# A diffusion transformer block in one kernel: the first MLP's latent tokens by Strassen's seven block products as well, the seven in a new order, and the sums of the second weights made inside each MLP

## The chip, the cores and the metric

The kernel runs on one core of a Trainium2 chip. The metric is device microseconds from start to end of one execution; three executions of the kernel before took 3232.7 to 3236.72 us, with a median of 3235.53. A profile of one execution (3236.36 us; its span from the first to the last instruction is 3234.6 us) gives the durations used below.

## The reference

Two layers work on 1024 latent tokens and 256 context tokens of width 1024, in fp32. Layer 0 mixes tokens by a long convolution and a windowed attention, layer 1 by latent attention and a Fourier mix. Behind each mixer comes an MLP, and only layer 0 goes on with the context:

```python
def _mlp(h, w1, w2):
    return jnp.square(jax.nn.relu(h @ w1)) @ w2

xl = _layer_norm(ALPHA * xl + g1 * yl, ln_g[l, 0], ln_b[l, 0])
xl = _layer_norm(ALPHA * xl + g2 * _mlp(_modulate(xl, sh2, sc2), mlp_w1[l], mlp_w2[l]), ln_g[l, 1], ln_b[l, 1])
if need_ctx:
    ...
    xc = _layer_norm(ALPHA * xc + g2c * _mlp(_modulate(xc, sh2c, sc2c), mlp_w1[l], mlp_w2[l]), ln_g[l, 1], ln_b[l, 1])
```

`w1` is 1024 x 4096 and `w2` 4096 x 1024. The gates and shifts come from `silu(c) @ mod_w[l]`, rows of 6 x 1024.

## The kernel before, in words

Every fp32 product is made of three TensorE passes on operands split in a high and a low part (`split`, L162 and L163: ScalarE rounds the high part, VectorE subtracts it for the low one; `mm3`, L169 to L171: high by high, low by high, high by low, into one PSUM bank). So each tile that TensorE reads costs ScalarE and VectorE one operation each.

Order: layer 0's mixer, `mixer_out` (output projection, residual, layer norm, tile by tile of 128 tokens), `Mlp`/`mlp`, layer 1's mixer (`MixerIn`, `mixer_cd_in`, `mla`), `mixer_out`, `FastMlp`. The instructions of each engine stand roughly in the order in which the program emits them; transfers are issued by SP (`nc.sync`) and by GpSimd (`nc.gpsimd`), each a queue in order. A tile pool with n buffers makes the writer of tile n+1 wait for the last reader of tile 1.

*The first MLP* (`mlp`, L1392) is plain. Its ten token tiles (eight latent, two context) go in two groups of five. For each group and each pair of 128-wide slices of the hidden width it loads and splits a slice of `w1` and of `w2`, makes the first layer with 320 moving columns (two halves of 640 tokens, 24 matmuls each), squares the relu, and makes the second layer with 512 columns for each token tile and half of the output, which VectorE adds up in SBUF (L1474). Beside it, `weight_sums` (L1547) makes four block sums of layer 1's `w2` for the second MLP and stores them to DRAM (`tsums`), and `mod_rows` (L348) builds layer 1's modulation, 128 multiply-adds on VectorE with their weights loaded by SP. Two steps before its end it makes `MixerIn`, which loads and splits the next mixer's weights, and `ahead` starts that mixer's projection between the last token tiles (`AHEAD`).

*The second MLP* (`FastMlp`, L1590) treats each matrix as 2 x 2 blocks and makes each 2 x 2 product by seven products instead of eight. The tokens' blocks are b11 to b22 and their sums t1 to t4 (`token_sums`), the weights' are a11 to a22 and s1 to s4. Its first layer goes by pairs of 128-wide hidden slices (`pairs`, L1734): 16 pairs, seven items each; an item is one split block of weights (128 x 512) and 12 matmuls of 512 columns. Three PSUM banks collect a pair's products, `a`, `x` and `y`; where a later item adds to a bank, VectorE has read it first. For the first `EARLY` = 7 pairs the items a11 b11 and a12 b21 are made ahead of all (`first`), while the token sums are still being formed; their results go to DRAM and are loaded again by the pair. `Stream` splits operands ahead of the multiplications, as far as a ring of `RING` = 6 places allows. Each pair ends with the squares and their four sums, all stored to DRAM (`sums`). The second layer (`passes`, L1844) goes product by product over the whole hidden width: seven times 16 items of 12 matmuls on four banks, one for each 128 tokens of a half, its operands loaded from `sums` and from `tsums` or `w2`. Residual and layer norm of each token half are put between the items (`aside`); the last product is finished tile by tile (`tail`).

Of the kernel before, what the change touches and what calls it, by code (L numbers as in the profile page):

```python
# [38 lines left out]
AHEAD = (1, 3, 4)  # L39
RING = 6  # L40
EARLY = 7
# [187 lines left out]
def setup(k, es):  # L229
# [23 lines left out]
    k.tsums = [dr.tile([128, 4, 2, 512], F32, name=f"tsums{j}") for j in range(8)]  # L253
    k.first = [dr.tile([128, 512], F32, name=f"first{j}") for j in range(EARLY)]
    k.erp = dr.tile([NH, 8, 31, 24], F32, name="erp")
# [455 lines left out]
def first_stage(k, hp, er):  # L711
# [4 lines left out]
    with ExitStack() as es:  # L716
# [27 lines left out]
        for j in range(1, 24):  # L744
# [24 lines left out]
            if extra and j in MODS:  # L769
                i, part = extra.pop(0)  # L770
                mod_rows(k, 0, i, 2, mr, ma, ph, "ph", cols=512, parts=(part,))
# [502 lines left out]
def mixer_out(k, l, y_of, weights, tiles, load_res, dst, streams, m):  # L1274
# [4 lines left out]
    with ExitStack() as es:  # L1279
        P = lambda n, b, **kw: es.enter_context(tc.tile_pool(name=n, bufs=b, reuse_waits="tile", **kw))  # L1280
        rw, rp = P("o_rw", 1), P("o_r", 2)
        if callable(weights):
            rs, sm, yb, w0, ya, w1, wr = P("o_rs", 2), P("o_sm", 4), P("o_yb", 1), P("o_w0", 1), P("o_ya", 1), P("o_w1", 1), P("o_wr", 4)
# [3 lines left out]
        else:  # L1287
            ya, yb, sm, rs = P("o_ya", 1), P("o_yb", 1), P("o_sm", 4), P("o_rs", 2)
# [3 lines left out]
        for t in tiles:  # L1292
# [20 lines left out]
            if t == tiles[-1]:  # L1313
                m.head()
# [8 lines left out]
class Mlp:  # L1323


    def __init__(self, k, es, l, src, groups, streams):
        self.k, self.l, self.src, self.groups, self.streams = k, l, src, groups, streams
        R = lambda e, n, b: e.enter_context(k.tc.tile_pool(name=n, bufs=b, reuse_waits="tile", side="right"))
        self.nmax = max(len(g) for g in groups) * 128
        self.xp, self.tmp = R(es, "m_x", 3), R(es, "m_tmp", 1)  # L1330
        self.pt = es.enter_context(k.tc.tile_pool(name="m_pt", bufs=2, space=PSUM, reuse_waits="tile"))
        self.first = es.enter_context(ExitStack())
        self.wp1, self.hp = R(self.first, "m_w1", 2), R(self.first, "m_h", 1)
        self.R = R
        self.scsh = None
        self.hs, self.fed, self.ready = {}, [], []

    def runs(self, gi):

        k, g = self.k, self.groups[gi]  # L1340
        if self.scsh is None:
            self.scsh = [mod_sc_sh(k, self.l, 1, s) for s in range(self.streams)]
        if gi not in self.hs:
            self.hs[gi] = [[self.hp.tile([128, self.nmax], F32R, tag=f"{p}{i}", name="m_" + p) for i in range(KT)] for p in ("hi", "lo")]
        runs = []
        for t in g:
            s = 0 if t < 8 else 1
            if not runs or runs[-1][0] != s or len(runs[-1][1]) == 2:
                runs.append((s, []))
            runs[-1][1].append(t)  # L1350
        return runs

    def normed(self, t, src=None):

        nc = self.k.nc
        x = self.xp.tile([128, D], F32, tag="mx", name="mx")
        if src is None:
            nc.gpsimd.dma_start(out=x, in_=self.src[t])
        ln_apply(self.k, x, x if src is None else src, self.k.co[0, t])
        return x  # L1360

# [23 lines left out]
    def head(self):  # L1385
        pass
# [1183 lines left out]
```

## Time and profile before

| | us |
|---|---|
| median of three executions | 3235.53 |
| lowest, highest | 3232.7, 3236.72 |
| profiled execution | 3236.36 |
| its span | 3234.6 |
| TensorE busy in it | 3122.5 (97%) |
| VectorE busy in it | 2294.5 (71%) |
| ScalarE busy in it | 1429.5 (44%) |

| stretch, us | what runs |
|---|---|
| 880 to 1007 | output projection of layer 0's mixer |
| 1007 to 1910 | first MLP |
| 1910 to 1990 | its last tiles, start of layer 1's mixer |
| 2488 to 2587 | output projection of layer 1's mixer |
| 2587 to 2640 | second MLP: items made ahead, token sums |
| 2640 to 2906 | its pairs |
| 2906 to 3235 | its second layer and the end |

PE is TensorE's matmuls, PEld its weight loads, DVE is VectorE, ACT ScalarE, POOL GpSimd. Matmuls are recorded with their whole passage, so neighbours overlap; the pace is read from start to start. An idle engine costs nothing unless TensorE waits for it.

### The profile page before, as it was taken

Reading aid. Unit: us, or ns where it says so; the run is one execution under the profiler, and the core shown is the slowest. Engines: PE = TensorE matmul, PEld = TensorE weight load, DVE = VectorE, ACT = ScalarE, POOL = GpSimd, SP = SyncE. Lnnn points to the kernel's source line nnn. Section 1 sums busy time; section 2 is a strip of 40 time slices with the busy share of each in tenths; the row PEclk is TensorE's granted clock in tenths of the full one; section 3 lists DMA queues with packets and bytes.
Section 4 is the critical chain, followed back from the end, with each engine's and each line's share of the span. In section 5 each row is a group of like instructions: output and inputs, shape, how many; then the busy total and the mean of one; then the engine's idle time right before and its main releaser. Section 6 shows DMA issues by size and latency. Waiting matters only on the chain. (4 is left out here: it accounts for less than half of the span.)

```text
span 3234.6 us, 47247 instructions
## 1 busy us (share of the span) xinstructions
PE 3122.5 (97%) x17700; PEld 2671.1 (83%) x17700; DVE 2294.5 (71%) x4231; ACT 1429.5 (44%) x2917; POOL 334.8 (10%) x525
## 2 busy tenths in 40 slices
PE   8999998999999999999999999999999999999998
PEld 4888886887778899888989987888888777888887
DVE  6777765888687777558555477687777886665668
ACT  3443333555543332235333334566666254444452
POOL 2100001222121000002000013100000212210001
PEclk9999998999999999999999999999999999999999
DMA  7434445332256676434434233200003355446564
GB/s 259 144 123 143 140 160 165 95 118 84 92 187 201 212 232 210 144 104 153 139 100 124 84 119 116 92 12 13 17 16 119 119 188 190 156 156 218 210 240 155
DMA packets 308786, 449.06 MB, mean 139 GB/s; under 512 B 26981, under 2 KB 208011, under 8 KB 308044
## 3 DMA queue, kind: packets, MB, share of 16 engines
q1 hardware_dynamic: 279004, 345.42, 33.1%
q0 software_dynamic: 29552, 100.62, 8.9%
q8 instruction: 139, 2.28, 0.3%
q14 instruction: 91, 0.75, 0.1%
HBM read 343.36 MB, written 104.26 MB: 138 GB/s over the span
## 5 line engine op out<-in xcount | busy, mean ns | idle before, releaser
L170 PE MATMUL mm<-m_lo,w1h 128*128 128x320 f32 x1024 | 316.7, 310 | 0.1
L169 PE MATMUL mm<-m_hi,w1h 128*128 128x320 f32 x1024 | 316.8, 310 | 0.0
L171 PE MATMUL mm<-m_hi,w1l 128*128 128x320 f32 x1024 | 316.1, 309 | 0.7 <-DVE w1l L163 0.7
L169 PE MATMUL mm<-w2h,ah 128*128 128x512 f32 x640 | 257.3, 402 | 10.4 <-DVE acc L1474 10.4
L171 PE MATMUL mm<-w2h,al 128*128 128x512 f32 x640 | 250.9, 392 | 0.0
L170 PE MATMUL mm<-w2l,ah 128*128 128x512 f32 x640 | 250.4, 391 | 0.0
L1474 DVE TENSOR_TENSOR acc<-mm,acc 128x512 f32<-128x512 f32 x270 | 183.9, 688 | 88.1 <-PE mm L171 86.9
L169 PE MATMUL pj<-hTh,hwh 128*128 128x512 f32 (+1 forms) x576 | 208.2, 362 | 0.0
L170 PE MATMUL pj<-hTl,hwh 128*128 128x512 f32 (+1 forms) x576 | 206.8, 360 | 0.3 <-DVE hTl L220 0.3
L171 PE MATMUL pj<-hTh,hwl 128*128 128x512 f32 (+1 forms) x576 | 206.6, 359 | 0.3 <-DVE hwl L163 0.3
L314 DVE SCALAR_TENSOR_TENSOR modacc<-modraw,silu,modacc 128x512 f32<-128x512 f32 x224 | 160.9, 747 | 47.5 <-DMA modraw<-in_mod_w 47.1
L169 PEld LDWEIGHTS mm<-m_hi,w1h 128*128 128x128 f32 x1024 | 192.2, 188 | 2.6 <-ACT m_hi L219 0.5
L170 PEld LDWEIGHTS mm<-m_lo,w1h 128*128 128x128 f32 x1024 | 192.2, 188 | 2.2 <-DVE m_lo L220 0.6
L171 PEld LDWEIGHTS mm<-m_hi,w1l 128*128 128x128 f32 x1024 | 192.1, 188 | 1.3 <-DVE w1l L163 1.0
L162 ACT CAST w2h<-wraw 128x1024 fp32r<-128x1024 f32 x64 | 64.5, 1047 | 265.7 <-PE mm L171 262.5
L163 DVE TENSOR_TENSOR w1l<-wraw,w1h 128x1024 fp32r<-128x1024 f32 x64 | 78.4, 1224 | 119.1 <-ACT w1h L162 119.0
L169 PEld LDWEIGHTS mm<-w2h,ah 128*128 128x128 f32 x640 | 120.8, 189 | 35.5 <-DVE acc L1474 14.6
L163 DVE TENSOR_TENSOR m_pl<-m_sl,m_ph 128x512 fp32r<-128x512 f32 x104 | 71.7, 690 | 101.0 <-ACT m_ph L162 101.0
L171 PEld LDWEIGHTS mm<-w2h,al 128*128 128x128 f32 x640 | 120.5, 188 | 25.3
L170 PEld LDWEIGHTS mm<-w2l,ah 128*128 128x128 f32 x640 | 120.9, 189 | 20.7
L2399 ACT ACTIVATE a_p<-a_s,a_m 128x512 f32<-128x512 f32 (+1 forms) x192 | 116.1, 614 | 44.2 <-DVE a_m L2395 43.5
L162 ACT CAST w1h<-wraw 128x1024 fp32r<-128x1024 f32 x64 | 67.1, 1049 | 138.6 <-PE mm L170 71.8
(1317 smaller groups left out, 9096.5 us busy)
## 6 DMA issues: line engine op xcount, KB each, us to landing
wraw<-in_mlp_w SPq DMA_DIRECT2D x128, 512.0 KB
modraw<-in_mod_w SPq DMA_DIRECT2D x160, 256.0 KB
m_sl<-sums SPq DMA_DIRECT2D x56, 512.0 KB
m_w<-in_mlp_w SPq DMA_DIRECT2D x39, 512.0 KB
m_ts<-in_mlp_w SPq DMA_DIRECT2D x16, 1024.0 KB
tsums<-m_ts POOLq DMA_DIRECT2D x16, 1024.0 KB, 5.0
sums<-m_s POOLq DMA_DIRECT2D x64, 256.0 KB, 3.7
m_sr<-tsums SPq DMA_DIRECT2D x32, 512.0 KB
```

Of the source, the lines that this page charges most:

```text
L162: nc.scalar.copy(hi, src)
L163: nc.vector.tensor_tensor(out=lo, in0=src, in1=hi, op=ALU.subtract)
L169: t.matmul(out, lh, rh, start=start, stop=False, skip_group_check=on)
L170: t.matmul(out, lh, rl, start=False, stop=False, skip_group_check=on)
L171: t.matmul(out, ll, rh, start=False, stop=stop, skip_group_check=on)
L314: k.nc.vector.scalar_tensor_tensor(out=acc, in0=w, scalar=c, in1=acc, op0=ALU.mult, op1=ALU.add)
L1474: nc.vector.tensor_tensor(out=acc[t][:, e], in0=ps, in1=acc[t][:, e], op=ALU.add)
L2399: nc.scalar.activation(out=p_[:, s:s + n], in_=ss[i][:, :n], func=AF.Exp, bias=m, scale=-1.0, accum_out=acc[:, i:i + 1])
```

## The change

The class `Mlp` with `mlp` and the function `weight_sums` are removed; `FastMlp` serves both layers. For layer 0 the latent tokens go through the seven products; the context's first layer is plain (256 columns), its squares and their block sums go to DRAM (`sumc`), and its second layer joins the seven products as a fifth token tile. In the pairs an item s1 t1 opens bank `y` (behind a11 b11 on `a` where that was not made ahead) and s4 b22 adds to it (behind a12 b21 on `a`); s2 t2, s3 t3 and a22 t4 go to `x`. The lists `five`, `three`, `six`, `seven` and `four` hold these, and a pair's `six`, `seven`, `four` alternate with the next pair's `five` and `three`. The seven products of the second layer follow the order of `PRODUCTS`. Each MLP makes its own sums of `w2`, in half units of 128 x 4 x 256 on the buffers of the token tiles, between its pairs. `EARLY` goes from 7 to 6. In `mixer_out` for layer 0 the residual's pools move to the right side of SBUF, and the weights' and operands' pools are closed at the last tile, where `head` opens the ring in their place. Layer 1's modulation is put between the context's steps and the first products of the second layer; `MixerIn` is made 13 items before the end.

```diff
-AHEAD = (1, 3, 4)
-EARLY = 7
+EARLY = 6
...
 def mod_rows(k, l, j, streams, raw_pool, acc_pool, pp, tag, tags=("wraw", "modacc"), cols=D, parts=(0, 1)):
...
                 mac(k, acc[s], w, k.silu[:, kt, s:s + 1], kt == 0)
+                yield True
...
 def mixer_out(k, l, y_of, weights, tiles, load_res, dst, streams, m):
-            rs, sm, yb, w0, ya, w1, wr = P("o_rs", 2), P("o_sm", 4), P("o_yb", 1), P("o_w0", 1), P("o_ya", 1), P("o_w1", 1), P("o_wr", 4)
+            rw, rp, rs, sm = (P(n, b, side="right") for n, b in (("o_rw", 1), ("o_r", 2), ("o_rs", 2), ("o_sm", 4)))
+            Q = lambda n, b: ops.enter_context(tc.tile_pool(name=n, bufs=b, reuse_waits="tile"))
+            wr, ya, yb, w0, w1 = Q("o_wr", 4), Q("o_ya", 1), Q("o_yb", 1), Q("o_w0", 1), Q("o_w1", 1)
...
             if t == tiles[-1]:
+                ops.close()
                 m.head()
...
-PRODUCTS = ("a11 b11", "a12 b21", "s2 t2", "s3 t3", "a22 t4", "s1 t1", "s4 b22")
+PRODUCTS = ("a11 b11", "a12 b21", "s1 t1", "s4 b22", "s2 t2", "s3 t3", "a22 t4")
+OPENS = (0, 2, 4)
...
+    def weight_sums(self):
+        k, tt = self.k, self.k.nc.vector.tensor_tensor
+        w2 = k.mlp_w2[self.l].rearrange("(j t p) (d c n) -> j c p t d n", t=2, p=128, d=2, c=2)
+        for j in range(FF // 256):
+            for c in range(2):
+                w = self.xp.tile([128, 4, 256], F32, tag="mx", name="m_ts")
+                for t in range(2):
+                    k.nc.sync.dma_start(out=w[:, 2 * t:2 * t + 2], in_=w2[j, c, :, t])
+                b11, b12, b21, b22 = (w[:, i] for i in range(4))
+                for out, a, b in ((b11, b12, b11), (b12, b22, b12), (b22, b22, b11), (b21, b21, b22)):
+                    tt(out=out, in0=a, in1=b, op=ALU.subtract)
+                    yield True
+                k.nc.gpsimd.dma_start(out=k.tsums[self.l][j // 2][:, :, j % 2, c * 256:c * 256 + 256], in_=w)
...
+                count[0] += 1
+                self.aside(1 + (count[0] % 3 == 0))
...
+            def after5():
+                if early:
+                    p.e, p.c = new("e"), new("c")
+                    nc.sync.dma_start(out=p.e, in_=k.first[j])
+                    nc.sync.dma_start(out=p.c, in_=k.sums[0, j // 2][:, j % 2])
+                p.f, p.g = new("f"), new("g")
+                add(p.f, p.y, p.e)
...
-        ps[0].six()
-        for j, p in enumerate(ps):
-            for f in p.front:
-                f()
-            if j + 1 < len(ps):
-                ps[j + 1].six()
-            for f in p.back:
-                f()
+        items = ps[0].five + ps[0].three
+        for p, q in zip(ps, ps[1:]):
+            items += p.six + q.five + p.seven + q.three + p.four
+        return items, ps[-1]
...
+            def multiply(*ws):
+                state[odd] = self.bank("c")
+                for i, w in enumerate(ws):
+                    h, l_ = (p.rearrange("p (k m) -> p k m", k=4) for p in w)
+                    for kt in range(4):
+                        mm3(k, state[odd][:, :LC], h[:, kt], l_[:, kt], self.xch[:, i * 4 + kt], self.xcl[:, i * 4 + kt], i + kt == 0, i + kt == 4)
+                        weave(k)
...
+        def multiply(i, j, m, a, b, *c):
+            if m < 4:
+                s = slice(m * 128, (m + 1) * 128)
+                h, l_ = a[0][:, s], a[1][:, s]
+            else:
+                h, l_ = c[0]
+            mm3(k, banks[m], h, l_, *b, i in OPENS and j == 0, j == nj - 1, i not in OPENS)
+            weave(k)
...
+        self.add(p.six + follow[:1] + p.seven + follow[1:2] + p.four)
+        self.hook(first_done)
+        self.add(follow[2:])
+        n = -(FF // 256) + 3 if self.then else 0
+        self.add(second[:n or None] if self.ctx else second[2:])
+        if self.then:
+            self.hook(next_stage)
+            self.add(second[n:])
...
+        for i in range(nm):
+            if i % 2 == 0:
+                self.ahead()
+            for _ in self.ends[i]:
+                pass
```

## Rows read from the trace of the kernel before

**Rows 1.** Page, part 1: busy us of an engine, share of the span, instructions.

```profile
PE 3122.5 (97%) x17700; PEld 2671.1 (83%) x17700; DVE 2294.5 (71%) x4231; ACT 1429.5 (44%) x2917; POOL 334.8 (10%) x525
```

**Rows 2.** Table by stretch, first MLP: stretch, length, busy of each engine (count), clock, DMA.

```profile
1007.00:1910.00 903.00, 891.73 (x5072) 810.41 (x5072) 577.30 (x845) 319.52 (x584) 37.52 (x50) 1.00 0.47 151
1030.00:1330.00 300.00, 291.78 (x1648) 264.30 (x1647) 210.96 (x310) 101.09 (x178) 10.69 (x15) 0.99 0.65 215
1910.00:1990.00 80.00, 71.85 (x343) 59.95 (x342) 71.98 (x181) 36.95 (x91) 27.83 (x47) 0.96 0.44 140
```

**Rows 3.** Table by stretch, second MLP.

```profile
2587.00:2630.00 43.00, 41.49 (x190) 33.59 (x188) 35.50 (x58) 25.54 (x49) 10.15 (x17) 1.00 0.66 208
2630.00:2640.00 10.00, 7.48 (x30) 5.96 (x29) 10.00 (x18) 6.14 (x11) 1.08 (x2) 0.83 0.25 97
2640.00:2740.00 100.00, 91.47 (x385) 72.56 (x384) 72.40 (x118) 41.61 (x72) 18.89 (x35) 0.98 0.61 195
2740.00:2906.00 166.00, 166.00 (x724) 135.62 (x723) 110.24 (x173) 83.04 (x139) 33.48 (x62) 1.00 0.46 154
2906.00:3200.00 294.00, 294.00 (x1296) 242.67 (x1295) 180.86 (x281) 136.16 (x241) 9.41 (x16) 1.00 0.62 217
```

**Rows 4.** Timeline of TensorE, first MLP: start us, duration us, instruction.

```profile
1201.18 0.31 PE L169 MATMUL mm<-m_hi,w1h 128*128 128x320 f32 x1
...
1201.91 0.31 PE L171 MATMUL mm<-m_hi,w1l 128*128 128x320 f32 x1
```

**Rows 5.** Timeline of TensorE, matmuls of 256 columns.

```profile
229.35 0.28 PE L521 MATMUL f_h<-f_w3h,f_hid 128*128 128x256 f32 x1
...
229.82 0.28 PE L169 MATMUL f_z<-tab_fwlh,f_sdh 128*128 128x256 f32 x1
```

**Rows 6.** Page, part 5, first MLP's matmuls: busy us, mean ns, idle before.

```profile
L170 PE MATMUL mm<-m_lo,w1h 128*128 128x320 f32 x1024 | 316.7, 310 | 0.1
...
L169 PE MATMUL mm<-w2h,ah 128*128 128x512 f32 x640 | 257.3, 402 | 10.4 <-DVE acc L1474 10.4
```

**Rows 7.** Waits of TensorE, first MLP: us in total, times, longest us.

```profile
PE mm L169 <- DVE acc L1474: 10.4, 7, 3.4
```

**Rows 8.** Waits of TensorE, second MLP.

```profile
PE m_x L169 <- DVE m_v L1799: 8.1, 5, 2.7
```

**Rows 9.** Chain that ended last, second MLP: start us, us, what.

```profile
2627.02 0.60 DVE m_t32l L163
...
2692.78 5.06 DMA m_e<-first
```

**Rows 10.** Page, part 6: transfers, KB of one, median us to landing.

```profile
m_ts<-in_mlp_w SPq DMA_DIRECT2D x16, 1024.0 KB
tsums<-m_ts POOLq DMA_DIRECT2D x16, 1024.0 KB, 5.0
```

**Rows 11.** Instruction groups 900 to 1960: busy us, mean ns, idle before.

```profile
L314 DVE SCALAR_TENSOR_TENSOR modacc<-modraw,silu,modacc 128x512 f32<-128x512 f32 x112 | 81.2, 748 | 29.9 <-DMA modraw<-in_mod_w 29.7
...
L189 DVE BATCH_NORM_STATS2 bnst<-ra 128x6 f32<-128x512 f32 x76 | 49.1, 682 | 0.2
...
L220 DVE TENSOR_TENSOR m_lo<-modtmp,m_hi 128x256 fp32r<-128x256 f32 x32 | 13.5, 421 | 0.7 <-ACT m_hi L219 0.6
...
L1252 DVE SCALAR_TENSOR_TENSOR ra<-ra,bnmv,lng 128x512 f32<-128x512 f32 x8 | 5.8, 744 | 0.0
...
L200 DVE TENSOR_SCALAR mx<-ra,co 128x1024 f32<-128x1024 f32 x5 | 4.1, 813 | 3.0 <-POOL co L195 3.0
```

**Rows 12.** Table by stretch, two microseconds in which transfers fill the engines.

```profile
1022.50:1024.50 2.00, 2.00 (x18) 1.99 (x17) 1.46 (x3) 1.49 (x3) 0.00 (x0) 1.00 0.99 353
```

**Rows 13.** Waits of VectorE, first MLP.

```profile
DVE m_ts L1556 <- DMA m_ts<-in_mlp_w: 19.3, 11, 7.9
```

**Rows 14.** Table by stretch, layer 0's output projection.

```profile
900.00:1007.00 107.00, 105.78 (x478) 84.09 (x477) 96.14 (x170) 32.71 (x67) 26.86 (x29) 1.00 0.50 161
```

**Rows 15.** Waits, 870 to 1012 us, GpSimd's queue.

```profile
POOL wrow L1267 <- DVE m L886: 14.2, 1, 14.2
```

More of the change, by code (lines that the diff above doesn't have):

```diff
@@ new lines, in after4 @@
+                late.extend([lambda: sums(0), lambda: sums(1), lambda: sums(2), lambda: sums(3)])
+            one = [] if early else [item(p, a11, "a", "b11", True, after1)]
+            two = [] if early else [item(p, lambda: p.a12, "a", "b21", False, after2)]
+            p.five, p.three = one + [item(p, s1, "y", "t1", True, after5)], two + [item(p, s4, "y", "b22", False, after3)]
+            p.six, p.seven, p.four = ([item(p, f, "x", b, b == "t2", g)] for f, b, g in ((lambda: p.s2, "t2", after6), (s3, "t3", after7), (lambda: p.a22, "t4", after4)))
@@ L1899, in item @@
-        def item(i, j):
-            def run(a, b):
-                if i in (0, 2, 5) and j == 0:
-                    banks[:] = [self.ps.tile([128, 512], F32, tag="ps", name=f"m_{'aaxxxyy'[i]}2") for _ in range(4)]
-                for m in range(4):
-                    multiply(i, j, m, a, b)
+            if i < 2:
+                nc.scalar.copy((b, a)[i][:, lo], ps)
+            elif i < last:
+                d, s = ((b, b[:, lo]), (a, b[:, lo]), (a, a[:, hi]), (b, b[:, hi]))[i - 2]
+                tt(out=d[:, hi], in0=ps, in1=s, op=ALU.add)
+            else:
+                self.tail(m, ps)
@@ L1931, in aside, with tile_of, gate @@
+    def tile_of(self, m, half):
+        return 8 + half if m == 4 else half * 4 + m
+    def gate(self, t):
+        return self.rows.g[0 if t < 8 else 1]
     def aside(self, n):
-        for _ in range(n):
-            if self.side and not next(self.side[0], False):
+        while n and self.side:
+            if next(self.side[0], False):
+                n -= 1
+            else:
                 self.side.pop(0)
     def residual_sum(self, t, a):
-        k, nc = self.k, self.k.nc
+        nc = self.k.nc
@@ L2021, in run @@
             self.whole.close()
+            e2.close()
             self.out = P(e1, "m_out", 1)
-            self.pairs()
-            while stream:
-                stream.step()
-            while self.late:
-                self.late.pop(0)()
-        self.inputs.close()
-        rw, rr, self.sm, self.kp = P(es, "m_rw", 1), P(es, "m_rr2", 1), P(es, "m_sm", 1), P(es, "m_kp", 1)
-        self.ra, self.rb = ([rr.tile([128, D], F32, name=f"m_r{c}{i}") for i in range(4)] for c in "ab")
-        self.st, self.side = {}, []
@@ new lines, in next_stage @@
+        def next_stage():
+            while self.side:
+                self.aside(1)
+            weave_rest(k)
+            self.free.close()
+            self.xcs.close()
+            self.ahead = self.then()
+        items, p = self.pairs()
+        second, rest = self.passes()
+        second = sum(second, [])
+        follow = self.context() if self.ctx else second[:2]
+        self.hook(all_tokens)
+        self.add(items)
+        if self.ctx:
+            self.hook(self.context_parts)
```

626 lines of the change are left out of this document (250 added, 376 removed).

## The prediction

> **What bounds the kernel now.** I read the page's busy shares first: TensorE is busy 97% of the span, the other engines far less [rows 1]. A busy TensorE can hide many short waits, so the next view is the table of engine busy time by stretch. In the first MLP, 1007 to 1910 us, TensorE is idle 11.3 us of 903, 8.2 of them between 1030 and 1330; the hand-over behind it, 1910 to 1990, idles 8.2 more [rows 2]. In the second MLP it is idle 1.5, 2.5 and 8.5 us in the three stretches up to 2740 and then not at all until the tail [rows 3]. So both MLPs cost what their matmuls cost at full pace, with small losses at the openings, and the granted clock is 1.00 in every undisturbed stretch, the upper of its two levels. What has to be read next is the pace, not the duration: the recorded matmuls overlap. From one start to the next a 320-column matmul takes 0.146 (0.73 us between two starts with four more in between, [rows 4]), a 256-column one 0.118 (0.47 us with three in between, [rows 5]), and a 512-column one 294 us / 1296 = 0.227 (the stretch 2906 to 3200, [rows 3]).
>
> **The change part by part.**
>
> *Matmuls of the first MLP.* Removed: the plain form, 3072 matmuls of 320 columns and 1920 of 512 [rows 6]: 3072 x 0.146 + 1920 x 0.227 = 448.5 + 435.8 = 884.3 us. Added: seven products for 1024 latent tokens, in each half 7 x 16 steps x 12 matmuls = 1344, together 2688 of 512 columns; the context's second layer rides in the same products as a fifth token tile, 7 x 16 x 3 = 336 of 512; the context's first layer is plain, 32 x 24 = 768 of 256. That is 3024 x 0.227 + 768 x 0.118 = 686.4 + 90.6 = 777.0 us. Transposes, gate rows and the modulation sums keep their numbers. Since TensorE is the bound of this stage, the difference counts in full: **-107 us**. A pace of 0.144 or 0.150 for the 320 columns would move it by -6 or +12.
>
> *Opening of the pairs.* The first MLP now opens as the second one does, which loses 12.5 us [rows 3]; its own old loss of 8.2, waits of the second layer for a PSUM bank that VectorE still had to add out [rows 7], goes. Net +4. In the second MLP most of the opening's waits, 8.1 us, are for VectorE's reading of bank x before the next product adds to it [rows 8]; the chain of work shows behind them the reload of a stored product, 5.06 us, which waits for its buffer [rows 9]. The new order asks first for t1 and b22, 16 of the 44 VectorE operations of the token sums, and leaves a product on another bank between two on x; but a reloaded product is now added to bank y with only one product (2.7 us) before the next on y, and its buffer still comes free late. I give the order -4 in the second MLP; its bounds are -12.5 (all waits gone) and +8 (two more microseconds for four of the early pairs).
>
> *Weight sums inside each MLP.* They were beside the first MLP: 16 loads and 16 stores of 1 MB [rows 10]. Now each MLP does its own in half units during the pairs: 32 units of four 256-wide subtractions, 128 x 0.42 = 54 us by the nearest row [rows 11], and two loads and a store of 512 KB a unit. VectorE is 110 us busy in the 166 us of undisturbed pairs, 66% [rows 3]; 54 us over some 290 add 19%, to 85%, and back to back its 512-wide operations follow each other every 0.60 us [rows 9], so it stays under the bound. Transfers: 33.6 MB more in 290 us is 116 GB/s on top of 154, 270 in all; the table shows 353 at a share of 0.99 [rows 12]. TensorE hides both if the waits stay short. A unit's first subtraction waits for its load in VectorE's queue, with the splits of the next products, which TensorE needs, behind it; now such waits sum to 19.3 us over the 16 units, 7.9 at most [rows 13]. The new unit is half as large and has two buffers, but the transfers are busier. Slack: the ring holds six products, 16 us, and VectorE has 15% free, 2.9 us a pair. I take +6 us for each MLP; bounds 0 and 50 (32 units at 1.6 us each with nothing hidden).
>
> *Context and modulation.* 30 plain context steps follow the pairs. Each reads 0.52 MB of first weights anew, stores half of 0.46 MB of sums and does one modulation step of 0.75 us [rows 11]: about 0.88 MB in 24 x 0.118 = 2.83 us, 312 GB/s, close to the 353 above. VectorE has two splits, the sums and that step, some 2.4 us. In the 49 second-layer steps after them two modulation steps each remain, 0.95 MB in 15 x 0.227 = 3.4 us, 279 GB/s. I take +8; bounds 0 and, if transfers ran only at the 217 GB/s of 2906 to 3200, 1.2 x 30 + 1.0 x 49 = 85.
>
> *End of the first MLP.* All five token tiles now end in the last step. VectorE then has 5 x 3 x 0.6 for the last halves, five normalisations of four 0.74 and two 0.68 operations [rows 11] and small ones, about 5 us each, and 8 for the next stage's inputs: 42 us. TensorE meanwhile has three tiles of the next stage's projection, 3 x 48 matmuls of 464 columns, an estimate of 0.21 each from the paces above: 30 us. 12 us open against 8.2 now: +4; bounds -8 (the next tiles, finished earlier, fill it) and +34 (nothing fills it).
>
> *Mixer output.* Five more tiles are normalised at once (0.81 each [rows 11], less the splits that the fifth tile no longer needs) where VectorE is 96 us busy of 107 [rows 14]: +2. The pools change sides; its first weights already wait 14.2 us in GpSimd's queue for the attention's last work [rows 15]. Taken as unchanged; bounds -4 and, if TensorE had to wait as long again, +14.
>
> *Sum.* -107 + 4 + 6 + 8 + 4 in the first MLP, -4 + 6 in the second, +2: -81. The profiled execution took 3236.4 (span 3234.6, and 1.8 around it), 0.8 above the median of 3235.5. 3236.4 - 81 = 3155 us.
>
> **The rivals.**
>
> *Waits vanish (18%).* The new order removes the second MLP's 12.5 us and, with it, the opening's loss in the first; the added work is hidden entirely. With the 8 for context and modulation kept, -107 - 8 - 12.5 + 8 = -120: 3117 us. For it: the steady pairs and second layer lose nothing now. Against it: more VectorE work and traffic in just those stretches.
>
> *Transfers take half (17%).* Context steps and modulation run at the mean rate of 250 GB/s: 0.88 / 0.25 = 3.5 us and 0.95 / 0.25 = 3.8 instead of 2.83 and 3.4, +21 and +20, so 3155 - 8 + 41 = 3188, up to 3205 with the pairs' traffic. For it: no long stretch here moves more than 217 GB/s. Against: a short stretch moves 353.
>
> *VectorE's queue becomes the bound (5%, slower).* If each of the 32 units a MLP holds VectorE for w us at its load, a pair has 2w less its 2.9 us of slack to pay, 32 pairs in the two MLPs. At w = 4 that is 5.1 x 32 = 163 us, less the 12 already counted: 3155 + 151 = 3306. It turns slower from 2w - 2.9 = 93 / 32, so w = 2.9 us on. The mean is 1.2 now [rows 13], in 1 MB units with one buffer. The Trainium skill says, on its page "SBUF — State Buffer", section "SBUF: two separate sides", that a transfer issued from GpSimd's queue stands still while VectorE holds the port the two share, because its descriptors can't be written. By that rule the stores, and with them the loads that wait for their buffers, come later just where VectorE is busiest; the trace's stores of 1 MB land in 5.0 us [rows 10] where VectorE is near 70% busy, so I do not raise the chance for it.
>
> **How the numbers follow.** Forecast 3155 with 58%, its own range 3132 to 3180; 3117 with 18%, 3188 to 3205 with 17%, slower with 5%, and 2% for a return to about the old time. Cutting a tenth at either end gives 3112 to 3205. What a measurement of this kernel can tell from no change is about 0.2%, 6.5 us: faster 0.93, same 0.02, slower 0.05.
>
> **What would show it.** Right: between the mixer's output and the hand-over some 3024 matmuls of 512 and 768 of 256 columns, at the paces above; the first MLP from 903 to about 820 us; the second within 10 us of its 635; VectorE near 85% and transfers near 270 GB/s in the pairs with TensorE idle under 5%. Wrong in a step: the waits of TensorE name VectorE's splits behind a wait for m_ts loads (weight sums), the context stretch is longer than 100 us (transfers), or the hand-over idles above 20 us (end). The forecast falls if TensorE's idle time in the two MLPs grows by more than 60 us.

## The result: slower, and the profile after

The changed kernel takes 3290.6 us (median of four, 3285.43 to 3295.35) against 3235.41 (four runs): a ratio of 1.0171, with a 95% interval of 1.0154 to 1.0189, so 55 us slower where 81 us faster were forecast. The profiled execution took 3291.76 us, its span is 3289.2. Four executions of the changed kernel lie 10 us apart; most experiments below are single executions, so a smaller difference of two totals among them says little.

TensorE does less, as forecast, and is idle more. Page, part 1, of the changed kernel, against [rows 1]:

```profile
PE 3067.3 (93%) x16500; PEld 2537.6 (77%) x16500; DVE 2409.1 (73%) x4712; ACT 1504.9 (46%) x3131; POOL 445.3 (14%) x704
```

3234.6 - 3122.5 = 112 us were idle before, 3289.2 - 3067.3 = 222 are now. The table by stretch says where; the columns are those of [rows 2]. The stretches are the first MLP's opening and pairs, its context steps, its second layer; then the second MLP's opening, its pairs, its second layer:

```profile
1018.00:1414.00 396.00, 343.77 (x1410) 269.61 (x1410) 287.84 (x521) 169.69 (x299) 94.58 (x161) 0.94 0.72 236
1414.00:1510.00 96.00, 90.45 (x740) 87.01 (x739) 80.88 (x170) 55.43 (x150) 14.75 (x17) 1.00 1.04 327
1510.00:1924.00 414.00, 403.87 (x1812) 330.55 (x1812) 299.93 (x554) 181.59 (x373) 21.93 (x30) 0.99 0.69 231
2580.00:2617.00 37.00, 35.08 (x160) 28.40 (x159) 32.53 (x54) 24.31 (x47) 8.04 (x13) 1.00 0.73 224
2617.00:2962.00 345.00, 303.65 (x1232) 240.22 (x1232) 248.81 (x455) 141.18 (x241) 81.86 (x140) 0.94 0.72 239
2962.00:3279.00 317.00, 304.87 (x1320) 247.25 (x1318) 199.94 (x313) 127.28 (x227) 10.91 (x15) 0.99 0.57 199
```

The two stretches of pairs stand out: TensorE idles 52 and 41 us in them, the granted clock is 0.94, and the transfers are busy 72% of the time at 236 to 239 GB/s, where [rows 3] had 154 to 195 GB/s. VectorE's 249 of 345 us are 72%: it is not full.

From the starts of the matmuls (first and last of each bank's) every run can be cut into the same five stretches. A: end of layer 0's projection. B: the first MLP up to the first score of the attention, with its first layer alone behind the slash. C: attention and projection. D: the second MLP's first layer and two steps of the second. E: the rest. The times are those of the profiled executions, the letters e1 to e18 name the experiments of the next section. In us:

| kernel | time | A | B | C | D | E |
|---|---|---|---|---|---|---|
| before | 3236.4 | 1008.8 | 1097.1 / - | 482.3 | 335.1 | 311.3 |
| changed | 3291.8 | 1017.9 | 1081.1 / 396.0 | 480.7 | 382.2 | 327.3 |
| no sums (e1) | 3189.8 | 1015.7 | 1030.5 / 347.4 | 480.9 | 333.5 | 327.4 |
| sums, no subtractions (e2) | 3289.7 | 1015.5 | 1090.7 / 402.4 | 481.6 | 377.0 | 323.0 |
| sums, no loads (e3) | 3221.4 | 1017.8 | 1036.9 / 354.5 | 482.8 | 354.7 | 327.1 |
| loads on GpSimd's queue (e4) | 3301.8 | 1014.6 | 1089.8 / 402.6 | 481.7 | 387.6 | 326.3 |
| transfers alone (e6) | 3325.6 | 1020.5 | 1099.2 / 414.0 | 482.6 | 396.7 | 324.9 |
| subtractions later (e7) | 3291.4 | 1019.1 | 1081.4 / 396.2 | 483.6 | 378.7 | 326.7 |
| old order (e8) | 3272.0 | 1019.2 | 1074.6 / 392.1 | 480.8 | 378.5 | 317.1 |
| transfers alone, held by VectorE (e9) | 3303.0 | 1020.6 | 1084.6 / 401.2 | 482.9 | 389.7 | 323.4 |
| four buffers (e10) | 3267.6 | 1020.5 | 1071.2 / 386.3 | 480.6 | 366.8 | 326.1 |
| half in the attention (e12) | 3293.6 | 1020.7 | 1077.6 / 392.8 | 511.5 | 357.1 | 324.5 |
| order and buffers (e17) | 3261.4 | 1020.1 | 1071.2 / 384.8 | 480.2 | 369.9 | 317.0 |

Changed against before: +9.1 in A, -16.0 in B, -1.6 in C, +47.1 in D, +16.0 in E, together 54.6, the difference of the spans.

What does a stall in the pairs look like? One from the second MLP's, first SyncE's queue, then VectorE, then TensorE (start us, duration us, instruction, idle before it and what ended it):

```profile
2696.22 1.21 SPq L1482 DMA_DIRECT2D m_ts<-in_mlp_w  x2
```

```profile
2692.25 0.42 DVE L1485 TENSOR_TENSOR m_ts<-m_ts 128x256 f32<-128x256 f32 x1
2699.33 0.76 DVE L1485 TENSOR_TENSOR m_ts<-m_ts 128x256 f32<-128x256 f32 x2 [6.66 <-DMA m_ts<-in_mlp_w]
...
2701.12 0.68 DVE L1569 TENSOR_TENSOR m_f<-m_x,m_f 128x512 f32<-128x512 f32 x1
```

```profile
2694.08 0.40 PE L169 MATMUL m_x<-m_t21l,m_ph 128*128 128x512 f32 x1
2701.86 0.80 PE L168 MATMUL m_x<-m_t40h,m_ph 128*128 128x512 f32 x1 [7.39 <-DVE m_f L1569]
2702.46 0.63 PE L169 MATMUL m_x<-m_t40l,m_ph 128*128 128x512 f32 x1
...
2706.30 0.43 PE L169 MATMUL m_y<-m_b221l,m_ph 128*128 128x512 f32 x1
```

A unit's load goes out late, VectorE stands 6.66 us at it, bank x is read late, TensorE idles 7.39 us. And the matmuls behind the pause start 0.43 apart instead of 0.23, up to 2706.30; the granted clock of that stretch is 0.53, so most of it ran at the lower of the two levels:

```profile
2701.80:2706.60 4.80, 4.74 (x12) 3.73 (x13) 4.80 (x10) 1.26 (x2) 2.73 (x5) 0.53 0.69 217
```

Ten starts take 4.44 us there instead of 2.3: the pause costs again over a quarter of its length. This is the rival "VectorE's queue" on the spot. Whether it is the cause is another question, and the experiments say no.

Over all of the second MLP's pairs, what TensorE, VectorE, ScalarE and SyncE's queue waited for (us in total, times, longest us):

```profile
PE m_x L168 <- DVE m_f L1569: 16.8, 6, 7.4
PE m_a L168 <- ACT m_e L1600: 10.2, 4, 4.2
...
DVE m_ts L1485 <- DMA m_ts<-in_mlp_w: 44.2, 22, 6.7
...
ACT m_e L1600 <- DMA sums<-m_e: 18.4, 7, 4.8
...
SPq L1482 <- DMA tsums<-m_ts: 131.9, 30, 9.3
```

Behind TensorE's largest wait stands VectorE at a load, four times in six one of the sums and twice one of first weights; behind the second stands a pair's own store, which holds the buffer that ScalarE wants. The unit's load itself waits on SyncE's queue until the store of two units before has landed.

### The profile page after: what moved, and what is told of

It reads as the page before. It is cut to its first block, busy times and chain, and to the rows that moved or that the text cites. A ratio compares the mean times of both kernels' runs of the same rounds, so it can differ in the third digit from the quotient of the medians.

```text
span 3289.2 us, 46932 instructions
## 1 busy us (share of the span) xinstructions
PE 3067.3 (93%) x16500; PEld 2537.6 (77%) x16500; DVE 2409.1 (73%) x4712; ACT 1504.9 (46%) x3131; POOL 445.3 (14%) x704
## 5 line engine op out<-in xcount | busy, mean ns | idle before, releaser
L161 ACT CAST m_ph<-m_sl 128x512 fp32r<-128x512 f32 x216 | 134.1, 621 | 352.9 <-PE m_y L169 114.8
L161 ACT CAST m_ph<-m_w 128x512 fp32r<-128x512 f32 x224 | 134.9, 615 | 199.1 <-DVE m_w L1591 70.4
L162 DVE TENSOR_TENSOR m_pl<-m_w,m_ph 128x512 fp32r<-128x512 f32 x224 | 152.5, 684 | 15.3 <-ACT m_ph L161 14.9
L162 DVE TENSOR_TENSOR m_pl<-m_sr,m_ph 128x512 fp32r<-128x512 f32 x216 | 147.9, 685 | 5.1 <-ACT m_ph L161 3.3
L169 PE MATMUL m_x<-m_pl,m_ph 128*128 128x512 f32 x352 | 140.0, 398 | 6.2 <-DVE m_pl L162 6.0
L168 PE MATMUL m_x<-m_ph 128*128 128x512 f32 x352 | 131.1, 393 | 8.8 <-ACT m_ph L161 6.1
L170 PE MATMUL m_x<-m_ph,m_pl 128*128 128x512 f32 x352 | 138.6, 394 | 0.0
L161 ACT CAST m_ph<-m_sr 128x512 fp32r<-128x512 f32 x216 | 133.6, 619 | 8.1 <-PE m_x L169 5.9
L168 PE MATMUL o_ps<-o_wh,yh 128*128 128x512 f32 x288 | 115.3, 403 | 10.4 <-ACT yh L161 10.4
L169 PEld LDWEIGHTS pj<-hTl,hwh 128*128 128x128 f32 x576 | 109.2, 190 | 17.5 <-DVE hTl L219 1.6
L169 PE MATMUL o_ps<-o_wl,yh 128*128 128x512 f32 x288 | 114.5, 399 | 0.0
```

Of the source, the lines that this page charges most:

```text
L161: nc.scalar.copy(hi, src)
L162: nc.vector.tensor_tensor(out=lo, in0=src, in1=hi, op=ALU.subtract)
L168: t.matmul(out, lh, rh, start=start, stop=False, skip_group_check=on)
L169: t.matmul(out, lh, rl, start=False, stop=False, skip_group_check=on)
L170: t.matmul(out, ll, rh, start=False, stop=stop, skip_group_check=on)
```

## The experiments

e1 to e11 each stand beside one execution of the kernel before (3232 to 3235 us), the others beside seven (3230 to 3242); e13, e16 and e18 have four executions themselves. Theory A at the start was that rival; against it stood the new order of the pairs' items (B) and the transfers themselves or one queue (C). An ellipsis in a code block marks lines left out.

**e1: no weight sums.** The passes that need sums read a plain block of `w2`.

```
- self.side = (turns if self.ctx else []) + [self.weight_sums()]
+ self.side = turns if self.ctx else []
...
- in_=k.tsums[self.l][j // 2][:, RIGHT[r]]
+ in_=w2[:, j // 2 * 2:j // 2 * 2 + 2, 0, HALVES[0]]
```

> Leaves out the block sums of the second weights in both MLPs (loads, subtractions, stores); the second layer reads a plain block of w2 in their place, the same number of transfers of the same size. Theory A (the sums between the pairs stop VectorE's queue at their loads, and TensorE starves): the pairs of each MLP fall from about 348 us to 275-290, the total from 3290 to 3150-3175. Rival B (the new order of the pairs' seven items, with its buffers, is what costs): the pairs stay above 330, total 3260-3290. Rival C (transfers as such, or SP's queue): the same as A; runs 2 to 4 part A from C.

3189.75 us, 15 above theory A's range: the sums cost 101 us, 48.6 in the first MLP's first layer and 48.7 in D. (The loads, stores and subtractions are gone together here; the next runs part them.) Rival B falls, for the second MLP's pairs take 298 us and not over 330. Without the sums the change is 45 us faster than before, not 93 as the forecast without its 12 us for the sums would have it. The second MLP's opening and pairs without sums:

```profile
2527.00:2861.00 334.00, 321.30 (x1396) 260.04 (x1395) 241.06 (x379) 170.41 (x287) 66.20 (x121) 0.99 0.52 171
```

**e2: loads and stores of the sums, no subtractions.**

```
  for out, a, b in (...):
-     tt(out=out, in0=a, in1=b, op=ALU.subtract)
      yield True
```

> Keeps the sums' loads and stores, leaves out their subtractions (what is stored is what was loaded), so VectorE never waits for these loads. Theory A: most of the loss goes, pairs 280-300, total 3165-3200. Rival C (bandwidth, or SP's queue that stands at a load which waits for a store, with the first weights behind it): the pairs stay at 330-350, total 3260-3290. VectorE's plain work (54 us of operations a MLP) as the cause: as A.

3289.66: nothing gained. Theory A falls. VectorE waits for no load of the sums any more, these loads go out sooner (in the second MLP between 2608 and 2801 us, against 2600 to 2880 in the changed kernel), and other late transfers take over (waits in the second MLP's first layer: us in total, times, longest):

```profile
PE m_y L168 <- DVE m_f L1568: 25.6, 3, 13.2
DVE m_f L1568 <- DMA m_e<-first: 24.4, 4, 14.2
ACT m_e L1599 <- DMA sums<-m_e: 23.7, 7, 10.2
```

Here it is the reload of a product made ahead, and the store that must leave a pair's buffer e before ScalarE writes the next.

**e3: subtractions (on a resident tile) and stores, no loads.**

```
+ still = k.ident.unsqueeze(1).to_broadcast([128, 2, 128])
...
- for t in range(2):
-     k.nc.sync.dma_start(out=w[:, 2 * t:2 * t + 2], in_=w2[j, c, :, t])
...
- tt(out=out, in0=a, in1=b, op=ALU.subtract)
+ tt(out=out.rearrange("p (a b) -> p a b", a=2), in0=still, in1=still, op=ALU.subtract)
```

> Keeps the subtractions (on a resident tile) and the stores, leaves out the sums' loads. Theory A (the wait for the load): pairs 280-300, total 3170-3200. VectorE's plain work as the cause: pairs stay above 325, total above 3245. SP's queue as the cause: as A, since no load stands in it.

3221.36, between the two expectations. Of the sums' 48.6 and 48.7 us the loads' absence gives back 41.5 in the first MLP and 27.5 in the second; VectorE works as in the changed kernel, and 7 and 21 us remain with the subtractions and the stores.

**e4: the sums' loads on GpSimd's queue.** `k.nc.sync.dma_start` becomes `k.nc.gpsimd.dma_start` for them.

> The sums' loads go from SP's queue to GpSimd's, in which the stores already are; nothing else changes. If SP's queue, standing at a load that waits for a store, holds the first weights up (SP waited 132 us so in the pairs of the second MLP): pairs fall to 290-310, total 3200-3230. If VectorE's own wait for the sums' load is what costs: no gain or a little, pairs 335-355, total 3270-3300.

3301.82, no gain: D is 387.6 against 382.2. That SyncE's queue stands at these loads (131.9 us of waits in the second MLP's pairs, for the buffer that a unit's store holds) is not by itself the cost.

**e6: the same transfers, nothing waits for them.**

```
+ there = self.xp.tile(...)   # zeros, stored each time
+ w = self.xp.tile(...)       # loaded each time, never read
  for j in range(FF // 256):
      for c in range(2):
          ...                 # the two loads into w
          for _ in range(4):
              yield True
          k.nc.gpsimd.dma_start(out=k.tsums[...], in_=there)
```

> Leaves the weight sums out but moves their bytes: the same loads (into one tile that nobody reads) and the same stores (out of a tile of zeros), from the same queues at the same pace; no load waits for a store, no store for a load or a subtraction, and the products that use the sums read zeros. Theory W (waits): the cost of the sums is one unit's load, subtractions and store waiting for one another in queues that are served in order, with the pairs' own transfers and splits behind them: 3195 to 3220, near the 3190 of the kernel without sums. Rival T (traffic): the bytes themselves cost it, because the pairs' own loads and stores land later beside them: 3265 to 3295, like the kernel without subtractions (3290).

3325.64, above rival T's range and worse than the changed kernel. Theory W falls in this form, but the run was no clean test: with no wait to hold them the loads ran ahead, and this splits the first layer in two halves (the table by stretch):

```profile
2602.00:2800.00 198.00, 132.15 (x530) 103.30 (x528) 110.83 (x178) 67.89 (x119) 51.14 (x80) 0.84 0.88 294
2800.00:2999.00 199.00, 199.00 (x867) 162.36 (x866) 130.05 (x201) 101.92 (x167) 39.93 (x74) 1.00 0.49 163
```

All loads lie in the first half: 294 GB/s, TensorE idle for 66 us. In the second, at 163 GB/s, it is idle for none. VectorE's busy share is 56% where TensorE idles and 65% where it doesn't.

**e9: the same, paced.** VectorE writes two words of `w` ahead of each unit's loads.

> Leaves the weight sums out but moves their bytes, as the transfers alone did, with one thing more: VectorE writes two words of the loads' tile at the start of each unit, so that a load can't run ahead of the program (in the run before, the loads bunched at 6 to 10 in 20 us, and the 78 us of gaps between the matmuls of the second MLP's pairs lay where they did). No store waits for a load, no load for a store. Theory W (the unit's load, subtractions and store wait for one another through two buffers, with the pairs' own transfers behind them): 3190 to 3225. Rival T (67 MB more in the two stretches of pairs, whatever waits for whom): 3265 to 3295.

3302.97, above T's range too: the bytes alone cost as much as the sums, without any unit's load, subtractions and store in a chain. (The pacing is not free of waits: VectorE's two words waited 45 us for the load before. In e6 they are absent and the price is higher.) But the pace is not the changed kernel's. In the second MLP the loads go out between 2640 and 2838 us and the stores between 2610 and 2711, against 2600 to 2880 and 2634 to 2887 there, and TensorE idles where the loads are and not behind them:

```profile
2640.00:2840.00 200.00, 149.81 (x588) 117.11 (x589) 106.88 (x228) 64.82 (x111) 38.98 (x67) 0.88 0.81 267
2840.00:2977.80 137.80, 137.80 (x601) 112.55 (x600) 90.32 (x140) 70.90 (x118) 28.54 (x53) 1.00 0.50 168
```

So e2, e6 and e9 show what these bytes cost in some 175 to 200 us; that they would cost as much alone, spread over 280 us as in the changed kernel, no run shows.

**e7: subtractions two steps after the load.**

```
+ yield True
+ yield True
  for n, (out, a, b) in enumerate(...):
...
```

> The whole computation, the same transfers at the same pace; a unit's subtractions are issued two steps after its load instead of with it, so that neither VectorE nor GpSimd's queue stands at a load on its way. Theory W: most of the 48 us that the sums cost in each of the two MLPs comes back, 3215 to 3255. Theory T: 3280 to 3295.

3291.41, no change. VectorE still waits 41.7 us for these loads: they go out when their buffer is free, not when the program would have them.

**e10: four buffers for the units instead of two.**

```
+ self.tsp = P(e1, "m_tsp", 2)
...
- w = self.xp.tile([128, 4, 256], F32, tag="mx", name="m_ts")
+ w = (self.tsp if (2 * j + c) % 4 >= 2 else self.xp).tile([128, 4, 256], F32, tag="mx", name="m_ts")
```

> The whole computation; the sums' units take turns in four buffers instead of two (two more 4 KB tiles, during the pairs alone). Theory W: the SyncE queue no longer stands at a unit's load for the store of two units before (131.9 us in the second MLP's pairs, the longest wait there), the reloads and weight loads behind it come in time: 3225 to 3265. Rival T: 3283 to 3297. Below both, if the loads now run ahead and bunch: over 3297.

3267.56, between the two expectations: 9.7 us back in the first MLP's first layer, 15.4 in D, a quarter of the sums' price. Buffers soften late transfers; they don't make them early.

**e11: a third buffer for the tile e.** `bufs=3` for it, 2 for f, g and c as before.

> The whole computation; the tile e of a pair (from which it is stored and to which the next pairs' first product is copied) has three buffers instead of two, the sums' units two as before. Theory S (the stores land late, and the copy of a first product waits for the store out of its buffer, 18 us on ScalarE in each MLP, for which TensorE waits 7 to 10 us): the waits of the m_e copy for the store go, 3265 to 3282. Theories W and T, by which what is late is not this tile: 3284 to 3296.

3284.71, just within the range of W and T: 6.8 us in the first MLP's first layer, 0.9 in D. The waits for that store are gone from TensorE's list, and others are longer.

**e12: half of layer 1's sums in the attention**, where the transfers are busy 4 to 5% of the time, subtracted on GpSimd; the other half is spread over all the pairs.

```
+ if h == 4 and g == 1: sums = early_sums(k, 1, ...)     # units j < 8
...
  next(run.pop(0) if c == "s" else pend, None)
+ next(sums, None)
...
- for j in range(FF // 256):
+ for j in range(0 if self.ctx else 8, FF // 256):
...
- self.aside(1 + (count[0] % 3 == 0))
+ self.aside(1 + (count[0] % 3 == 0) if self.ctx else int(count[0] % 3 > 0))
```

> Half of layer 1's weight sums (16 of 32 units) move out of the second MLP's pairs into two heads of the attention of layer 1, where the transfers are busy 4 to 5% of the time; their subtractions run on GpSimd there. The other half is spread over all the pairs. Theory T (the price is the bytes moved beside the pairs' own): the second MLP's pairs fall from 345 us to 318 to 328 (halfway to the 297 without sums) and the attention stretch, 370.3 us from its first score to its last, grows by no more than 6: 3263 to 3278. Rival (a price in each unit, wherever it runs: buffers, queues, subtractions): the attention grows by what the pairs give back, 3283 to 3297.

3293.61. D gives back 25.1 us, half the price for half the bytes, as theory T has it; but the attention grows by 31, as the rival has it. The longest wait of VectorE in those heads:

```profile
DVE a_ob L2403 <- DMA ycd<-a_ob: 25.2, 3, 16.1
```

The attention's own result goes out on SyncE's queue, behind a load of the sums that waits for its buffer, and VectorE can't write the next result.

**e15: that store on GpSimd's queue. e18: two buffers for the result as well** (on top of e16).

```
- nc.sync.dma_start(out=k.ycd[g][h * 96:(h + 1) * 96, :], in_=ob)
+ (nc.gpsimd if 4 <= h < NH - 1 else nc.sync).dma_start(out=k.ycd[g][h * 96:(h + 1) * 96, :], in_=ob)
...
- ob = qf_.tile([96, 256], F32, tag="ob", name="a_ob")
+ ob = qf_.tile([96, 256], F32, tag="ob", name="a_ob", bufs=2)
```

> Half of layer 1's sums in the attention once more, with one change: in those heads the attention's own result a_ob goes out on GpSimd's queue, so that it doesn't stand on SyncE's behind a load of the sums that waits for its buffer (in the run before VectorE waited 25.2 us for that store, 16.1 of them at once, of the 31 us by which the attention grew). If it was that queue, the attention grows by 4 to 10 instead of 31, while the second MLP's first layer stays at some 357 us (382 in the changed kernel): 3265 to 3276. Rival (each unit has its price wherever it runs, the queue only showed it): the attention grows by 20 or more again, 3284 to 3297.

> The combined kernel before it (3268) with one edit: the attention's result a_ob has two buffers, so that a head's result need not have left before the next is written (VectorE waited 23.9 us for that store in the attention, 12.8 at once, with the store behind the sums on GpSimd's queue). If the price of the half in the attention is that wait, the stretch from the attention's first score to the projection behind it falls from 405 us to 382 to 390, and the kernel to 3242 to 3254. If the sums have their price wherever they run, it stays at 400 or more and the kernel at 3260 to 3272.

From the first score to the projection the attention took 381.5 us in the changed kernel, 412.4 in e12, 406.6 in e15 (3282.54), 405.4 in e16 and 399.0 in e18. In e15 it still grows by 25, which is the rival's side (20 or more), with a time 1.5 us below the rival's range; e18 lies between its two expectations by the attention, and its 3260.54 within the range of a price wherever the sums run. The price shrinks as the store is freed, and 17.5 us remain, with the same wait at the head of VectorE's list, for on GpSimd's queue the store stands behind subtractions that wait for their loads:

```profile
DVE a_ob L2412 <- DMA ycd<-a_ob: 16.2, 2, 12.4
```

So the largest wait seen in the attention is one store in a queue behind the sums. That the price would be nothing with that store alone on a queue was not shown, and a price of each unit wherever it runs is not excluded.

**e8: the second MLP's second layer in the order of before.**

```
+ BEFORE = ("a11 b11", "a12 b21", "s2 t2", "s3 t3", "a22 t4", "s1 t1", "s4 b22")
+ self.order = PRODUCTS if self.ctx else BEFORE
```

and there the residual work of one token half (`base`) comes behind the third product and of the other (`close`) behind the sixth.

> The second layer of the second MLP alone takes the seven products in the order of the kernel before (s2 t2, s3 t3, a22 t4, s1 t1, s4 b22 after the first two), so half of the residual work comes after the third product and not all of it behind the fifth and sixth. Theory (end): the 15 us of gaps between the matmuls of the last third (splits late behind residual work on VectorE) shrink to a few, the last product group of 576 or 384 matmuls runs without gaps over 0.5 us: 3273 to 3282. Rival (the gaps come from late loads, not from VectorE): 3286 to 3295.

3271.98, 1 us below the theory's range: 10.2 us back in E, as the theory has it, and 8 more in stretches that it doesn't touch (3.9 in the first MLP's first layer, 3.7 in D), for which one execution gives no reason. In the new order half of the residual work of the eight tiles comes behind the fifth product and half behind the sixth, and VectorE's splits come late (the changed kernel's last group of products, then the same stretch of this one):

```profile
3180.00:3250.00 70.00, 58.36 (x235) 43.75 (x233) 64.10 (x100) 24.52 (x44) 6.51 (x9) 0.98 0.68 233
```

```profile
3168.00:3257.00 89.00, 88.09 (x386) 71.68 (x384) 72.73 (x121) 28.06 (x50) 6.71 (x8) 1.00 0.53 182
```

**e5: layer 0's projection with five pools in the old order**, `ya, yb, w0, w1, wr` instead of `wr, ya, yb, w0, w1`.

> Only the order of five pools in the first output projection goes back: w0, w1 and the raw weights behind ya and yb, so that the raw tiles no longer stand where the result of the long convolution is read last. Theory (pools): the first o_ps matmul comes some 10 us earlier against the stage before it (after: 10.5 us of the 55 lie there), the time is 3276 to 3284, unless MLP 1's ring, which then lies on other tiles, starts later by as much. Rival (the new slices of the projection themselves cost it): 3286 to 3295, no change.

3293.83, and A ends at 1016.6 against 1017.9: no gain, the theory of that pool falls. Its first four raw weights have all landed at 883.8 us (881.6 before, 893.6 in the changed kernel), yet ScalarE splits the first of them at 892.4 (882.5 before); why was not followed further.

**e13, e14, e16, e17: together.** e14 has the old order, four buffers and layer 0's sums at three quarters of the pace, the rest behind the context; e13 adds the half in the attention. e17 has order and buffers at the changed kernel's pace; e16 adds the half in the attention with its own queue.

> Together: half of layer 1's sums in the attention, four buffers for the sums' units, layer 0's sums at three quarters of the pace with the rest behind the context's stage (none beside it), the second MLP's second layer in the order of the kernel before. If the prices found add up (19 for the order, 23 for the buffers, some 24 for the half in the attention, 5 to 10 for the slower pace): 3205 to 3225, faster than the kernel before (3235). If they overlap, as the buffers' and the place's may: 3225 to 3245, the same as before.

> The combined kernel without the half in the attention: all of layer 1's sums beside the second MLP's pairs, in four buffers. If the prices add up, 20 to 28 above the combined kernel, 3230 to 3250; if the buffers alone take what the place takes, within 8 of it.

> Together: that half in the attention with its own queue, four buffers for the sums' units in both MLPs at the changed kernel's pace, and the second MLP's second layer in the order of before. Stage by stage from the runs so far: first MLP's first layer 386 (buffers), attention +4 to +10, second MLP 670 (as in the first combined kernel): 3232 to 3248, the same as the kernel before within its 0.5%. If the attention grows by 20 or more again: 3250 to 3265.

> The second MLP's second layer in the order of before and four buffers for the sums' units, both at the changed kernel's pace, nothing in the attention. If the two add up (10 in the second layer and 4 to 8 beside it; 10 and 15 in the two first layers): 3248 to 3262. If the slower pace and not the place behind the context cost the gain of the buffers in the first MLP in the kernel without the attention (396 against 386 us): the first MLP's first layer takes 383 to 389 us here.

3285.63 (ratio 1.0147, 1.0128 to 1.0165), 3273.98, 3268.22 (1.0101, 1.0084 to 1.0118) and 3261.4; e18 took 3260.54 (1.0083, 1.0064 to 1.0103). The first three are above all that was expected of them, e13 by 40 us and more; only e17 lies in its range. The slower pace gained nothing and lost the buffers' gain in the first MLP (395.8 and 398.0 against 386.3 us in e10; 384.8 in e17). Order and buffers together give 29 us from the changed kernel, less than the 19 + 23 that they gave singly. No version that makes the sums beats the kernel before: in e17 the two first layers still take 384.8 and 369.9 us against 347.4 and 333.5 without sums.

## Why the prediction was wrong

136 us lie between forecast and result. By its terms:

*Weight sums: +12 forecast, 101 measured, 89 of the 136.* This is the step that failed. The prediction asked whether the transfers' mean (270 GB/s expected, 236 to 239 found) stays under the 353 of [rows 12], saw that it does, and took the waits from the old units' 19.3 us in [rows 13]. A mean under the maximum did not make the transfers early: e2 shows that the sums cost the same without VectorE's work and waits, e3 that without their loads 69 of the 97 us come back; e6 and e9 show that the bytes, with no chain of waits but in a shorter time, stall TensorE as much as the sums do; e1 and the second half of e6 show that TensorE hardly stalls at 163 to 171 GB/s. The slack was counted on the wrong resource too. VectorE had 28% left, but a pair stores and reloads through one or two buffers, and most of its stores land later. Issues in the second MLP's pairs, KB each and median us to landing, in the changed kernel, then in e1:

```profile
sums<-m_s POOLq DMA_DIRECT2D x63, 256.0 KB, 4.5
...
sums<-m_e POOLq DMA_DIRECT2D x17, 256.0 KB, 4.4
sums<-m_f POOLq DMA_DIRECT2D x16, 256.0 KB, 3.2
```

```profile
sums<-m_s POOLq DMA_DIRECT2D x63, 256.0 KB, 3.6
...
sums<-m_e POOLq DMA_DIRECT2D x17, 256.0 KB, 4.4
sums<-m_f POOLq DMA_DIRECT2D x16, 256.0 KB, 2.3
```

The stores of e don't land later by the median, nor do those of c (2.7 against 2.6), so the landing times alone don't make up the price. The bound of 50 us a MLP, 32 units at 1.6 us with nothing hidden, is near the 48.6 and 48.7 that came, but by luck: 1.6 us is about what a unit's four subtractions of 0.42 us take, and e2 has none of them and costs the same.

The rival "VectorE's queue becomes the bound" had the sign and half of the sight: the units' waits at their loads are there (44.2 us in the second MLP's pairs), but taking them away (e2) or giving the loads more time (e7, where 41.7 us of them stay) changed nothing, and its size, 3306 us, came near by another mechanism. The page of the Trainium skill cited with it, "SBUF — State Buffer", section "SBUF: two separate sides", says that GpSimd can't write a transfer's descriptors while VectorE runs an operation in a 2-port mode; the prediction took that as true of all of VectorE's work. No run here tests the page's rule itself. The prediction's reading of it is not borne out: e2, with VectorE 240 us busy in D instead of 281, is no faster as a whole (D 5 us shorter, the first MLP's first layer 6 longer), and the stores of zeros in e9 land in 8.2 us with VectorE 243 us busy, against 4.7 in the changed kernel. Another page of the Trainium skill fits better: "DMA: Bandwidth & Descriptors", section "Issuing engines are not separate DMA queues", says that transfers of all issuing engines run on the same 16 engines and interleave; e4, which only changes the issuer, agrees (387.6 against 382.2).

The rival "transfers take half" named the right resource and priced mainly the context and the modulation, with 17 us at most for the pairs, and there the forecast held: the context steps took 95.2 us at 327 GB/s, under the 100 set as its sign, and TensorE idled 5.5 of them. As far as the trace shows, nothing is stored there that a later step's bank waits for.

*Matmuls: -107, right.* The recorded matmuls are 3024 of 512 columns in the first MLP and 768 in the context's first layer; one starts every 0.2275 us, and between 1510 and 1840 TensorE has no gap.

*New order, second layer: not priced, +16.* The prediction followed the new order in the pairs alone. -4 there is nearly right (D is 333.5 without sums against 335.1), but the order also moves the second layer's residual work, half of which lay behind the third product before, to the end: E is 16.0 us longer. e8 gives 10.2 back.

*Opening of the first MLP: +4, about 21.* A gap is what the starts of two matmuls lie apart beyond 0.2275 us, counted where they are 0.40 or more apart, so it holds pauses and slowed matmuls. Without the sums TensorE's gaps in opening and pairs are 29.6 us, against the 12.5 of [rows 3] that the forecast carried over; the old 8.2 go.

*Context and modulation: +8, about 5*, the idle time of the context steps (5.5 us, 4.4 without sums). *End of the first MLP: +4, about 15.* From 1840 to 2000 TensorE is idle 20 us of 160, on the prediction's mark of 20, with 6.8 at once for VectorE's next input tile; in gaps between matmuls that is 24 us (25 in e1) against 10 before, over 80 us. *Mixer output: +2, about 7 in e1 and 9 in the changed kernel*, within its bounds: the first matmul of o_ps starts at 895.4 instead of 883.6, which the pools' order alone doesn't explain (893.4 in e5).

Against the forecast these are 89 + 16 + 17 - 3 + 11 + 5 and 2 in D, together 137.

What the prediction set as its own failure, 60 us more idle time in the two MLPs, came: about 100.

## What to carry to other kernels

Work that moves bytes beside a tuned stage is not hidden because the engines and the mean bandwidth have room. Look in that stage at what is stored and loaded again through one or two buffers, and price the added bytes there by a run that moves them at the pace of the real work and does nothing else. An order of products has a second price, at the end, where the last sums and their residual work come together: follow a new order through every stage that uses it.

## What was not expected of the hardware

In these first layers TensorE waits for transfers long before they fill the 16 engines. At a share of 0.52 to 0.54 (171 to 173 GB/s, e1) a first layer runs with 16 and 30 us of gaps between the matmuls, mostly in its first 150 us; at 0.62 (208, e3) with 36; at 0.70 to 0.74 (233 to 247) with 49 to 75; at 0.88 (294) two thirds of the time was left for TensorE. The share alone does not decide it: the second layer before ran at 0.62 (217) with no idle time [rows 3], and the context steps at 327 GB/s with 5.5 us in 96. Which of the transfers comes late changes with each edit, the sum less: D was 377.0, 378.7, 382.2, 387.6 and 389.7 us in five versions that move the same bytes, 366.8 with four buffers and 396.7 where the loads ran ahead. What makes them late, the engines, the memory, the queues or the 1 KB pieces of these units, was not separated.

And a pause of TensorE costs more than its length: in D of the changed kernel 29 pauses make 50 us, and 67 further matmuls start 0.40 to 0.50 us apart instead of 0.23, 13 us more, at a granted clock of 0.95 against 0.99 without the sums.
